# Four of the first layer's six modulation vectors as weighted sums on VectorE, spread over the attention phase, in place of TensorE products

## Chip, cores and metric

One NeuronCore of a Trainium2 chip. The metric is the device time of one execution in microseconds; lower is better. The kernel runs in float32 throughout; its large products are made of three products of float32r parts.

## What is computed

Two layers over 512 latent and 256 context tokens of width 1024. Each layer is modulated by six vectors, made from the conditioning `c` (for the latent tokens) and `c_ctx` (for the context):

```python
for layer in range(DEPTH):
    mod_x = silu_c @ ada_w[layer] + ada_b[layer]      # 1024 -> 6 x 1024
    mod_c = silu_cc @ ada_w[layer] + ada_b[layer]
    sh1, sc1, g1, sh2, sc2, g2 = split(mod_x, 6)
    hx = modulate(rmsnorm(x, norm1_g[layer]), sh1, sc1)
    mx, mc = hybrid_mixer(hx, hc, ...)                # projections, two kinds of attention heads, gates
    x = x + g1 * (mx @ w_out[layer])
    hx = modulate(rmsnorm(x, norm2_g[layer]), sh2, sc2)
    x = x + g2 * squared_relu_mlp(hx, w_mlp1[layer], w_mlp2[layer])
```

and the same for the context in the first layer. The first two vectors (shift and scale of the first norm) are wanted at the start; the third only when the mixer's output is projected, the fourth and fifth at the second norm, the sixth at the end of the MLP's first part. The change concerns these last four, in the first layer.

## The kernel before

Tokens lie on the free axis, 128 features on the partitions. `build` makes a list of items, layer by layer, and `run` (L400) emits them in order; each engine then works through its own queue in that order, so the list is the schedule. Ahead of every item, and behind each one that uses weights, `advance` (L409) emits loads and splits of the next weight slabs: a slab of 128 x 1024 is loaded on SP's queue into one of four buffers of the pool `wraw`, and split into a high part (a cast on ScalarE, L244) and a low part (a subtraction, L245, on VectorE or, for a few slabs, on GpSimd). There are six pairs of split buffers (`NSPL`): a slab's split can be emitted only when the slab six places before it in the order of use has had its last use (L413).

The attention phase follows the hand-written table `SCHEDULE` (L109): 24 lines with one block of projections each, and the stages that run behind it. Its first eighteen lines begin

```python
vg0 g0A g2A g1A      # 1        gk1 g1O g0N g3B      # 8       ka1 r13 r01          # 15
vg1 g0B g1B g2B      # 2        qa0 g2qk g1N g3C     # 9       kb1 r1N r02          # 16
vg2 g1C g2C g0C      # 3        qb0 g2S g2K g3qk     # 10      g5 r03 r31           # 17
vr0 g0qk g1qk        # 4        ka0 g3S g3K g2D      # 11      g1 r32 r0N y5        # 18
vr1 g0S g0K g1S      # 5        kb0 g3D g2O          # 12
vr2 g0D g1K tabs     # 6        qa1 g3O g2N r11      # 13
gq1 g1D g0O g3A      # 7        qb1 r12 g3N          # 14
```

(the numbers are this document's). A block is some 48 to 144 matmuls and the evacuation of its banks; `vg` and `vr` (values, token-major, `tok_blocks` L735) use four slabs in all three of their blocks, slabs 5 to 8 and 9 to 12. A stage of the gated linear attention is a step of one head: A to C make the gate's prefix sums (VectorE and ScalarE), `qk` scales queries and keys (VectorE), S and K make scores and transposes (TensorE), D the states over the chunks (TensorE, then VectorE), O the output, N its norm. The retention heads' stages are r..1 to r..N.

The modulation vectors are made in three ways. Shift and scale of the first layer come first, in four quarters (L374). The first layer's other four vectors come in two groups of 2048 features: `ada_step` (L279) multiplies, for one of eight k tiles, four stretches of 512 columns of the raw weights by the conditioning's column pair (32 stationary columns, 30 of them zero), side by side in four strips of the array; with `ada_load` two raw slabs are loaded a step ahead. `ada_next` (L306) is placed behind each block of the schedule (L1132): 16 steps, behind the blocks 1 to 16. At a group's end `ada_finish` (L259) copies the bank to SBUF, transposes it on TensorE and adds the bias on VectorE. The second layer's six vectors are made by `ada_sums` (L324) during the first layer's MLP: for each k tile VectorE adds the raw slab, weighted by a per-partition scalar, to an accumulator, once for each of the two conditionings (L340 for the first k tile, L342 for the others); after eight tiles one product with a one-hot column adds up the partitions (L348), and `ada_finish` follows. Its accumulator shares a buffer with the retention tables (`tag="rtab"`).

```python
for v in range(2):
    c = cs[:, kk, v : v + 1]
    if kk == 0:
        nc.vector.tensor_scalar(acc[:, v], w, c, None, op0=ALU.mult)
    else:
        nc.vector.scalar_tensor_tensor(acc[:, v], w, c, acc[:, v], op0=ALU.mult, op1=ALU.add)
```

Of the kernel before, what the change touches and what calls it, by code (L numbers as in the profile page):

```python
# [16 lines left out]
P = 128  # L17
# [22 lines left out]
class Item:  # L40
    """A piece of the program: emits instructions; may need weight slabs; a stage runs one block after its deps."""
# [5 lines left out]
class Chains:  # L47
    """Instruction chains that hop between engines: each tick emits the next step of every chain under way.

    Queued chains start one per tick, with at most WIDTH of them under way."""  # L50
# [45 lines left out]
class Act:  # L96
    """A moving operand in two float32r parts, made by chains for token ranges."""
# [10 lines left out]
# one block of projections and the attention stages that run behind it, per line; at most NSLOT tiles live  # L108
# [30 lines left out]
def build(ctx: ExitStack, tc, a):  # L139
# [7 lines left out]
    tp = ctx.enter_context(tc.tile_pool(name="tab", bufs=1))  # L147
    mp = ctx.enter_context(tc.tile_pool(name="mp", bufs=NSLOT))
# [23 lines left out]
    def bc(col, n):  # L172
        """[P, c] -> [P, c, n], each value repeated n times."""
        return col.rearrange("p (c o) -> p c o", o=1).to_broadcast([col.shape[0], col.shape[1], n])

    def rep(tab, c):
        """[P, n] -> [P, c, n], the row repeated c times."""
        return tab.rearrange("p (o t) -> p o t", o=1).to_broadcast([tab.shape[0], c, tab.shape[1]])
# [5 lines left out]
    # ---- constants and inputs  # L184
# [32 lines left out]
    # silu(c) of both vectors, as 32 stationary columns (30 of them zero) per k tile  # L217
# [14 lines left out]
    # ---- weight slabs: [128, 1024] and its exact split into two float32r parts  # L232
# [14 lines left out]
    class RankSlab(Slab):  # L247
        """Four copies of 32 columns per k tile: the second one's low part, the others' high parts."""
# [7 lines left out]
    # ---- adaLN vectors: mod[l][p, v, j] for feature 128 j + p  # L256
    mod = [const.tile([P, 2, 48], F32, name=f"mod{l}") for l in range(DEPTH)]

    def ada_finish(l, pt, tiles, n, fold=1):  # L259
        """pt: row 32 c + v holds, for vector v, n features from the tile tiles[c] on; `fold` such parts are summed."""  # L260
# [18 lines left out]
    def ada_step(state, l, g, kk):  # L279
        if kk == 0:  # L280
            state["pt"] = psa.tile([P, 512], F32, tag="psa", name=f"ada_{l}_{g}")
        pt = state["pt"]
        w = state.pop("w", None)
        if w is None:
            w = ada_load(l, g, kk)
        for c in range(4):
            nc.tensor.matmul(
                pt[32 * c : 32 * c + 32, :], cs[:, kk, :], w[c // 2][:, (c % 2) * 512 : (c % 2 + 1) * 512],
                start=(kk == 0), stop=(kk == KK - 1),
            )  # L290
        if kk == KK - 1:
            state["end", l, g] = ch.start(ada_finish(l, pt, [16 * g + 4 * c for c in range(4)], 512))

    def ada_load(l, g, kk):
        ws = []
        for i in range(2):
            w = wraw.tile([P, WCOL], F32, tag="raw", name=f"adaw_{l}_{g}_{kk}_{i}")
            c0 = g * 2048 + i * WCOL
            nc.sync.dma_start(w, a["ada_w"][l, kk * P : (kk + 1) * P, c0 : c0 + WCOL])
            ws.append(w)  # L300
        return ws

    ada_state = {}
    ada_queue = [(l, g, kk) for l, g in ((0, 1), (0, 2)) for kk in range(KK)]

    def ada_next():  # L306
        if ada_queue:
            l, g, kk = ada_queue.pop(0)
            ada_step(ada_state, l, g, kk)
            if ada_queue:  # L310
                ada_state["w"] = ada_load(*ada_queue[0])

    def ada_drain(l, g):
        while any(q[:2] == (l, g) for q in ada_queue):
            ada_next()
        ch.finish(ada_state["end", l, g])

    # the second layer's: weighted sums over the k tiles on the vector engine, one product to add the partitions
# [5 lines left out]
    def ada_sums(l):  # L324
        acc = tp.tile([P, 2, WCOL], F32, tag="rtab", name=f"adaacc_{l}")
        todo = [(u, kk) for u in range(6) for kk in range(KK)]
# [8 lines left out]
        for i, (u, kk) in enumerate(todo):  # L335
# [8 lines left out]
            if kk == KK - 1:  # L344
# [7 lines left out]
                ada_state["end", l] = ch.start(ada_finish(l, pt, [8 * u + 2 * c for c in range(4)], 256))  # L352
                yield

    # the first layer's shift and scale, in four quarters of 256 features each
# [18 lines left out]
    def quarter(q, middle=None, end=None):  # L374
        """Shift and scale of a quarter, even and odd k tiles apart."""
# [65 lines left out]
    def project(pt, slab, c0, acts, t0, t1, ks=None, first=0, last=None):  # L441
        """pt[:, :t1 - t0] += W[:, tile].T @ act over the k tiles `ks` of a slab part [kk, 128]."""
# [14 lines left out]
    # ---- RMSNorm over features, for a group of tokens at a time  # L457
    class Norm:
# [3 lines left out]
        def square(self, kk, t0, t1, first):  # L462
            """A chain that adds a tile's squares to the sum."""
# [14 lines left out]
        def late_square(self, kk, t0, t1):  # L478
            """A tile's squares that the product over the partitions adds to the sum."""
            sq = temp(f"sq_{self.name}_{kk}_{t0}")[:, 0 : t1 - t0]  # L480
            nc.scalar.activation(sq, xs[kk][:, t0:t1], AF.Square)
            self.late.append(sq)
# [40 lines left out]
        def apply_all(self, l, shift, v, t0, t1, ks=range(KK)):  # L523
            """Chains that make the tiles `ks` of a group of tokens."""
# [910 lines left out]
```

## Time and profile before

| | us |
|---|---|
| median of three runs | 1659.46 |
| lowest, highest run | 1658.64, 1659.53 |
| span of the profiled execution, first to last instruction | 1658.9 |

The profile's time is its span; the runs shown lie from 0.3 below to 0.6 above it. PE is TensorE's matmul, PEld its weight load, DVE VectorE, ACT ScalarE, POOL GpSimd, SP the engine whose queue issues most loads. A granted clock of 1.00 is 2.4 GHz, 0.50 is 1.2 GHz. A row names the line of the program that made the instruction; where a helper records many operations, the tile names tell them apart (`ps_vr` is a bank of a `vr` block, `adaw` a raw slab of modulation weights, `lo_wi` a low part of an input-projection slab).

### The profile page before, as it was taken

The numbers are of one execution on the slowest core, as the hardware profiler recorded it, in microseconds if no ns is written. First come the engines' busy times: TensorE is split into PE (matmuls) and PEld (weight loads), VectorE is DVE, ScalarE is ACT, GpSimd is POOL, SyncE is SP. The second block draws the span as 40 slices with busy tenths as digits, with TensorE's granted clock in tenths as the row PEclk, the third lists the DMA queues.
The fourth block names the chain that finished last, engine by engine and source line by source line (L and its number), as shares of the span: only waits on it lengthen the run. The fifth ranks groups of instructions, "written<-read, shape, count | busy, mean of one in ns | idle before, by whom it ended". The sixth has DMA issues, their size and how long they took to land. (4 is left out here: it accounts for less than half of the span.)

```text
span 1658.9 us, 22890 instructions
## 1 busy us (share of the span) xinstructions
PE 1618.7 (98%) x9236; PEld 1384.2 (83%) x9236; DVE 946.9 (57%) x1491; ACT 629.5 (38%) x1083; POOL 201.6 (12%) x215
## 2 busy tenths in 40 slices
PE   5999999999999999999999999999999899999997
PEld 3778888888998888888888887888889888888887
DVE  5676664554755555555556476588466633443445
ACT  5535424562532222222212246363464532222232
POOL 3200021110111010110101121001110211010010
PEclk9999999999999999999999999999999999999999
DMA  9533433122323333333333222121123323223321
GB/s 323 175 127 126 137 108 102 39 88 90 103 89 127 115 127 109 120 102 116 126 115 127 95 88 66 51 77 52 51 89 128 103 89 102 91 100 102 102 64 51
DMA packets 57610, 173.80 MB, mean 105 GB/s; under 512 B 6208, under 2 KB 17792, under 8 KB 57504
## 3 DMA queue, kind: packets, MB, share of 16 engines
q1 hardware_dynamic: 55232, 164.85, 30.2%
q0 software_dynamic: 2272, 7.50, 1.2%
q8 instruction: 72, 1.18, 0.3%
q14 instruction: 34, 0.28, 0.0%
HBM read 168.13 MB, written 4.19 MB: 104 GB/s over the span
## 5 line engine op out<-in xcount | busy, mean ns | idle before, releaser
L437 PE MATMUL pm<-yh,hi_m 128*128 128x512 f32 (+1 forms) x800 | 279.6, 349 | 0.0
L437 PE MATMUL pm<-hidh,hi_m 128*128 128x512 f32 (+1 forms) x800 | 279.1, 349 | 0.0
L438 PE MATMUL pm<-yl,hi_m 128*128 128x512 f32 (+1 forms) x800 | 278.6, 348 | 0.0
L438 PE MATMUL pm<-hidl,hi_m 128*128 128x512 f32 (+1 forms) x800 | 278.4, 348 | 0.0
L439 PE MATMUL pm<-yh,lo_m 128*128 128x512 f32 (+1 forms) x800 | 278.2, 348 | 0.0
L439 PE MATMUL pm<-hidh,lo_m 128*128 128x512 f32 (+1 forms) x800 | 277.2, 347 | 0.0
L1208 ACT ACTIVATE relu<-pm 128x512 f32<-128x512 f32 (+1 forms) x100 | 51.1, 511 | 497.6 <-PE pm L439 493.9
L1212 DVE TENSOR_TENSOR hidl<-relu,hidh 128x512 fp32r<-128x512 f32 (+1 forms) x100 | 60.5, 607 | 296.0 <-POOL relu L1210 296.0
L1210 POOL TENSOR_TENSOR relu<-relu 128x512 f32<-128x512 f32 (+1 forms) x100 | 89.2, 893 | 760.3 <-ACT hidh L1209 760.2
L535 DVE SCALAR_TENSOR_TENSOR x<-pm,mod,x 128x512 f32<-128x512 f32 (+1 forms) x200 | 117.6, 640 | 106.6 <-PE pm L439 106.6
L437 PEld LDWEIGHTS pm<-yh,hi_m 128*128 128x128 f32 x800 | 152.6, 191 | 20.2 <-issue 1.2
L437 PEld LDWEIGHTS pm<-hidh,hi_m 128*128 128x128 f32 x800 | 151.5, 189 | 21.3 <-issue 1.1
L438 PEld LDWEIGHTS pm<-yl,hi_m 128*128 128x128 f32 x800 | 152.5, 191 | 18.8
L439 PEld LDWEIGHTS pm<-yh,lo_m 128*128 128x128 f32 x800 | 152.4, 191 | 19.0
L439 PEld LDWEIGHTS pm<-hidh,lo_m 128*128 128x128 f32 x800 | 151.1, 189 | 19.6
L438 PEld LDWEIGHTS pm<-hidl,hi_m 128*128 128x128 f32 x800 | 151.4, 189 | 18.9 <-issue 0.2
L245 DVE TENSOR_TENSOR lo_m<-raw_m,hi_m 128x1024 fp32r<-128x1024 f32 x126 | 154.0, 1222 | 10.6 <-ACT hi_m L244 10.6
L244 ACT CAST hi_m<-raw_m 128x1024 fp32r<-128x1024 f32 x128 | 129.6, 1040 | 51.6 <-DMA raw_m<-in_w_mlp 31.0
L342 DVE SCALAR_TENSOR_TENSOR adaacc<-adaw,cs,adaacc 128x1024 f32<-128x1024 f32 x84 | 103.9, 1278 | 0.0
L245 DVE TENSOR_TENSOR lo_wi<-raw_wi,hi_wi 128x1024 fp32r<-128x1024 f32 x49 | 60.6, 1249 | 29.8 <-ACT hi_wi L244 29.8
L437 PE MATMUL pwo<-yh,hi_wo 128*128 128x256 f32 (+1 forms) x224 | 70.9, 316 | 0.1
L438 PE MATMUL pwo<-yl,hi_wo 128*128 128x256 f32 (+1 forms) x224 | 70.3, 314 | 0.3 <-DVE yl L1056 0.3
(304 smaller groups left out, 2951.5 us busy)
## 6 DMA issues: line engine op xcount, KB each, us to landing
raw_m<-in_w_mlp SPq DMA_DIRECT2D x128, 512.0 KB, 3.5
adaw<-in_ada_w SPq DMA_DIRECT2D x80, 512.0 KB, 3.9
raw_wi<-in_w_in SPq DMA_DIRECT2D x58, 512.0 KB, 4.3
adaw<-in_ada_w SPq DMA_DIRECT2D x32, 256.0 KB, 6.3
raw_wo<-in_w_out SPq DMA_DIRECT2D x16, 512.0 KB, 3.4
x<-in_xT POOLq DMA_DIRECT2D x8, 384.0 KB, 7.8
x<-in_xT SPq DMA_DIRECT2D x8, 256.0 KB, 4.9
raw_wob<-in_w_out SPq DMA_DIRECT2D x4, 512.0 KB, 4.3
```

Of the source, the lines that this page charges most:

```text
L244: nc.scalar.copy(self.hi, self.raw)
L245: self.engine.tensor_sub(self.lo, self.raw, f32(self.hi))
L342: nc.vector.scalar_tensor_tensor(acc[:, v], w, c, acc[:, v], op0=ALU.mult, op1=ALU.add)
L437: nc.tensor.matmul(out, wh, xh, start=first, stop=False)
L438: nc.tensor.matmul(out, wh, xl, start=False, stop=False)
L439: nc.tensor.matmul(out, wl, xh, start=False, stop=last)
L535: nc.vector.scalar_tensor_tensor(xs[kk][:, t0:t1], pt[:, 0 : t1 - t0], mod[l][:, v, gate + kk : gate + kk + 1], xs[kk][:, t0:t1], op0=ALU. ...
L1208: nc.scalar.activation(r, pt[:, 0 : t1 - t0], AF.Relu)
L1210: nc.gpsimd.tensor_mul(r, r, r)
L1212: nc.vector.tensor_sub(a_.lo[:, t0:t1], r, f32(a_.hi[:, t0:t1]))
```

## The change

`ada_step` and `ada_load` go. `ada_sums` takes a list of vectors and makes the first layer's vectors 2 to 5 as well, its accumulator in a pool of its own (8 KB per partition; the descriptor scratch of the software DMA queue shrinks to 2 KB). `ada_next` runs its next step. There are nine steps to a vector: eight that emit a load for the step after and two sums, and one that emits the product over the partitions. A step is placed behind each block, as before, and one more at the end of each line of the schedule. `ada_drain` waits for one vector: the third ahead of the output projection, the fifth at the second norm, the sixth in the MLP's first part.

```diff
+    adap = ctx.enter_context(tc.tile_pool(name="adap", bufs=1))
...
-    def ada_step(state, l, g, kk):
-        if kk == 0:
-            state["pt"] = psa.tile([P, 512], F32, tag="psa", name=f"ada_{l}_{g}")
...
-        for c in range(4):
-            nc.tensor.matmul(
-                pt[32 * c : 32 * c + 32, :], cs[:, kk, :], w[c // 2][:, (c % 2) * 512 : (c % 2 + 1) * 512],
-                start=(kk == 0), stop=(kk == KK - 1),
-            )
...
-    ada_queue = [(l, g, kk) for l, g in ((0, 1), (0, 2)) for kk in range(KK)]
-
-    def ada_next():
-        if ada_queue:
-            l, g, kk = ada_queue.pop(0)
-            ada_step(ada_state, l, g, kk)
-            if ada_queue:
-                ada_state["w"] = ada_load(*ada_queue[0])
...
-    def ada_sums(l):
-        acc = tp.tile([P, 2, WCOL], F32, tag="rtab", name=f"adaacc_{l}")
-        todo = [(u, kk) for u in range(6) for kk in range(KK)]
+    def ada_sums(l, us=range(6)):
+        acc = adap.tile([P, 2, WCOL], F32, tag="acc", name=f"adaacc_{l}")
+        todo = [(u, kk) for u in us for kk in range(KK)]
...
-                ada_state["end", l] = ch.start(ada_finish(l, pt, [8 * u + 2 * c for c in range(4)], 256))
+                ada_state["end", l] = ada_state["end", l, u] = ch.start(
+                    ada_finish(l, pt, [8 * u + 2 * c for c in range(4)], 256)
+                )
                 yield
...
+    def ada_next():
+        if "sums0" not in ada_state:
+            ada_state["sums0"] = ada_sums(0, range(2, 6))
+        next(ada_state["sums0"], None)
+
+    def ada_drain(l, u):
+        while (l, u) not in [k[1:] for k in ada_state if k[0] == "end" and len(k) == 3]:
+            ada_next()
+        ch.finish(ada_state["end", l, u])
...
                 if it.slabs and l == 0:
                     plan.append(Item("ada", ada_next))
+            if l == 0:
+                plan.append(Item("ada", ada_next))
             seen.update(row)
...
-                        ada_drain(0, 2)
+                        ada_drain(0, 4)
...
-            plan.append(Item("ada1", lambda: ada_drain(0, 1)))
+            plan.append(Item("ada1", lambda: ada_drain(0, 2)))
...
+                if l == 0 and u == 0 and jps == [0]:
+                    ada_drain(0, 5)
...
-    nc = _bacc.Bacc("TRN2", target_bir_lowering=False, num_devices=1)
+    nc = _bacc.Bacc("TRN2", target_bir_lowering=False, num_devices=1, dynamic_dma_scratch_size=2048)
```

## Rows read from the trace of the kernel before

In order of time a row is: start in us, length in us, engine, line, operation, output and inputs by the program's names, partitions x elements and type, the number of instructions merged in it, and in square brackets the idle time before it with what ended it. In stretches a row is: start and end in us, their length, then for each engine the busy us and (x) the instructions in it, the granted TensorE clock as a share of 2.4 GHz, the DMA share and GB/s.

**Rows 1.** The page's busy line: us, share of the span, instructions.

```profile
PE 1618.7 (98%) x9236; PEld 1384.2 (83%) x9236; DVE 946.9 (57%) x1491; ACT 629.5 (38%) x1083; POOL 201.6 (12%) x215
```

**Rows 2.** Stretches behind blocks 2 to 8: busy us, granted clock, DMA.

```profile
88.29:100.40 12.11, 12.11 (x58) 9.09 (x57) 11.68 (x17) 1.55 (x8) 0.00 (x0) 1.00 0.27 87
100.40:112.50 12.10, 12.10 (x57) 9.09 (x56) 5.47 (x13) 10.28 (x17) 0.00 (x0) 1.00 0.52 180
112.50:124.61 12.11, 12.11 (x57) 9.09 (x56) 9.64 (x23) 0.00 (x0) 0.80 (x4) 1.00 0.47 168
124.61:140.59 15.98, 15.98 (x111) 12.56 (x110) 6.09 (x16) 4.69 (x8) 0.00 (x0) 1.00 0.21 67
140.59:152.14 11.55, 11.55 (x75) 9.59 (x74) 10.94 (x30) 8.44 (x23) 0.00 (x0) 1.00 0.51 184
152.14:166.02 13.88, 13.88 (x95) 11.92 (x94) 8.66 (x18) 9.40 (x18) 0.00 (x0) 1.00 0.46 148
166.02:179.97 13.95, 13.95 (x89) 11.47 (x88) 6.57 (x13) 6.57 (x13) 0.00 (x0) 1.00 0.24 80
```

**Rows 3.** TensorE's weight loads in block 4 (vr0), in order of time.

```profile
101.39 0.19 PEld L437 LDWEIGHTS ps_vr<-hi_wi,hh_n 128*128 128x128 f32 x1 [0.84 <-issue]
...
104.26 0.19 PEld L438 LDWEIGHTS ps_vr<-lo_wi,hh_n 128*128 128x128 f32 x1
```

**Rows 4.** TensorE's matmuls around two of the removed steps.

```profile
87.97 0.39 PE L439 MATMUL ps_vg<-hi_wi,hl_n 128*128 128x512 f32 x1
...
89.29 0.50 PE L437 MATMUL ps_vg<-hi_wi,hh_n 128*128 128x512 f32 x1
...
124.29 0.39 PE L439 MATMUL ps_vr<-hi_wi,hl_n 128*128 128x512 f32 x1
...
125.61 0.37 PE L857 MATMUL psf<-gq,gk 64*128 64x128 f32 x1
```

**Rows 5.** TensorE's matmuls around a product over partitions, second layer.

```profile
544.45 0.28 PE L439 MATMUL pm<-hidh,lo_m 128*128 128x256 f32 x1
...
545.65 0.50 PE L437 MATMUL pm<-yh,hi_m 128*128 128x512 f32 x1
```

**Rows 6.** VectorE's pair of weighted sums, second layer, and the next.

```profile
488.13 2.47 DVE L342 SCALAR_TENSOR_TENSOR adaacc<-adaw,cs,adaacc 128x1024 f32<-128x1024 f32 x2
490.52 1.22 DVE L245 TENSOR_TENSOR lo_m<-raw_m,hi_m 128x1024 fp32r<-128x1024 f32 x1
```

**Rows 7.** VectorE in order of time, behind blocks 1 to 4.

```profile
85.22 0.95 DVE L811 TENSOR_TENSOR gl<-gl,gt 128x768 f32<-128x768 f32 x1
...
99.35 0.96 DVE L821 TENSOR_TENSOR gt<-gt,gst 128x768 f32<-128x768 f32 x1
102.26 2.36 DVE L245 TENSOR_TENSOR lo_wi<-raw_wi,hi_wi 128x1024 fp32r<-128x1024 f32 x2 [1.95 <-ACT hi_wi L244]
...
120.30 0.68 DVE L757 TENSOR_REDUCE vsum<-ps_vr 128x4 f32<-128x512 f32 x1
...
121.22 1.13 DVE L760 TENSOR_SCALAR vr<-ps_vr,vsum 128x128 f32<-128x128 f32 x4
```

**Rows 8.** Stretches of 2 us around a stand of TensorE, second layer.

```profile
1292.00:1294.00 2.00, 0.73 (x7) 0.53 (x5) 1.52 (x4) 0.95 (x2) 0.00 (x0) 1.00 0.17 51
...
1296.00:1298.00 2.00, 0.84 (x3) 0.75 (x3) 2.00 (x2) 0.46 (x2) 1.58 (x2) 0.50 0.13 25
...
1302.00:1304.00 2.00, 2.00 (x17) 2.00 (x16) 1.75 (x5) 1.48 (x4) 0.00 (x0) 0.83 0.02 6
```

**Rows 9.** VectorE's last evacuation of qa0, TensorE's first matmul of qb0.

```profile
182.72 0.69 DVE L939 TENSOR_TENSOR rq<-ps_qa,c_sinT 64x512 f32<-64x512 f32 x1
...
182.18 0.58 PE L437 MATMUL ps_qb<-hh_n,hi_wi 128*128 128x512 f32 x1
```

**Rows 10.** VectorE's last evacuation of g1, TensorE's first matmul of g6.

```profile
303.01 0.42 DVE L1047 TENSOR_TENSOR sg<-se,ps_g 128x256 f32<-128x256 f32 x1 [0.48 <-ACT se L1046]
...
303.48 0.56 PE L437 MATMUL ps_g<-hh_n,hi_wi 128*128 128x512 f32 x1
```

More of the change, by code (lines that the diff above doesn't have):

```diff
@@ L277, in ada_finish @@
             )
-    def ada_step(state, l, g, kk):
-        if kk == 0:
-            state["pt"] = psa.tile([P, 512], F32, tag="psa", name=f"ada_{l}_{g}")
[L282 to L285, printed above, removed]
-        for c in range(4):
-            nc.tensor.matmul(
-                pt[32 * c : 32 * c + 32, :], cs[:, kk, :], w[c // 2][:, (c % 2) * 512 : (c % 2 + 1) * 512],
-                start=(kk == 0), stop=(kk == KK - 1),
-            )
[L291 to L301, printed above, removed]
-    ada_state = {}
-    ada_queue = [(l, g, kk) for l, g in ((0, 1), (0, 2)) for kk in range(KK)]
-    def ada_next():
-        if ada_queue:
-            l, g, kk = ada_queue.pop(0)
-            ada_step(ada_state, l, g, kk)
-            if ada_queue:
-                ada_state["w"] = ada_load(*ada_queue[0])
[L313 to L316, printed above, removed]
+    ada_state = {}
     onehot = const.tile([P, 2, 32], F32, name="onehot")
```

## The prediction, made before the change was built

> **What bounds the kernel now.** The page's busy line comes first: TensorE 98% of the span, VectorE 57% [rows 1]. Read alone, that says that work taken from TensorE and given to VectorE is a gain. An average over 1659 us can't be trusted here, since the change acts between 74 and 305 us only, so the second view cuts this stretch at the ends of the projection blocks. I number the blocks as the lines of SCHEDULE: vg0 is 1, vg1 2, vg2 3, vr0 4, vr1 5, vr2 6, and so on to g1, 18. In every piece TensorE is busy throughout at a granted clock of 1.00 (its 2.4 GHz level) and VectorE is not full [rows 2]: TensorE bounds this phase, and VectorE is ahead of it. But VectorE's share differs: 11.7 of 12.1 us behind block 2, 5.5 behind block 3, 10.9 of 11.6 behind block 6 [rows 2]. Where it is almost full, nothing more fits.
>
> **What goes.** Sixteen steps, one behind each of the blocks 1 to 16. The matmuls of a block follow each other by 0.22 us (13 of them between the two rows of [rows 3]). Around the step behind block 2 the distance is 89.29 - 87.97 = 1.32, so the step costs 1.1; where another plain float32 product follows, as behind block 5, it is 125.61 - 124.29 = 1.32 again, less the pace and some 0.1 for the change of format, which stays: 1.0 [rows 4]. Four steps of the first kind and twelve of the second: 4 x 1.1 + 12 x 1.0 = 16.4 us of TensorE, all on the path.
>
> **What comes.** Per vector a product over the partitions behind the sums: the second layer's same product moves the next matmul from 544.45 to 545.65, less the 256-column pace of 0.12, so 1.1 at most, 1.05 taken [rows 5]; four are 4.2. The transposes that follow are eight as before (four vectors by two, two groups by four): nothing. Alone, TensorE would end 16.4 - 4.2 = **12.2 us** earlier.
>
> VectorE gets 32 pairs of weighted sums. A pair holds it 490.52 - 488.13 = 2.4 us [rows 6]; the first pair of each vector is a plain product and cheaper, so some 28 x 2.4 + 4 x 1.4 = 73 us. Two steps come with each block: one right behind it, before the stages, and one behind the stages. With nine steps to a vector (eight sums, one product), all are spent with block 18.
>
> Priced at nothing: the 32 loads of 512 KB are 32 as before, now one to a step, on SP's queue; what hides them is that each is issued a step ahead, and if that cover were gone VectorE would wait some 4 us a step (the heavy rival below). The smaller descriptor scratch touches only POOL's DMAs, of which none is issued in this stretch; a delay of theirs would show at the start or where x is reloaded. The accumulator's own pool adds no instruction.
>
> **Who waits.** VectorE works its queue in order, so what stands behind the sums is late. I follow it by blocks. "Shift" is TensorE's time against before.
>
> *Block 4 (vr0), slabs 11 and 12.* They take the split buffers of slabs 5 and 6, which block 3 still reads; so their subtractions are emitted behind block 3, behind all of block 2's stages. Before, those stages run on VectorE without a gap from 85.22 to 99.35 + 0.96 = 100.3, and the two subtractions at 102.3 come just in time: vr0 begins at 101.39 and wants slab 11's low part at 104.26, less than a microsecond after it is made [rows 3, 7]. After: a sum behind block 1's stages, one behind block 2, 15.1 us of stages, one more sum, then the subtraction: 85.2 + 2.4 + 2.4 + 15.1 + 2.4 + 1.2 = 108.7. TensorE, three steps lighter, asks at 104.26 - 3.3 = 101.0. It stands **7.7 us** (bounds 6 and 9: whether the sums slip into small gaps or add some).
>
> *The clock.* In the second layer TensorE stood some 4.4 us (1292.7 to 1297.2 by the busy time); the granted clock was 0.50, the 1.2 GHz level, from then until about 1302.4 [rows 8]. 5.2 us of work at half rate gave 2.6 us away. A stand of 7.7 us is longer, so I take 2.6 again (bounds 0, if the clock holds, and 3.3, for the whole low stretch).
>
> *Block 5's product (vector 2).* From slab 12's subtraction, at 109.9, VectorE has what it had before in the pieces behind blocks 3 and 4 (5.5 - 2.4 and 9.6 less the 2.0 of vr1's first evacuation, together 10.8 [rows 2, 7]) and four sums, 9.6: free at 130.3. TensorE ends block 5 at 124.5 - 4.4 + 7.7 + 2.6 = 130.4. No stand here; had the clock held, it would be 2.5. Either way the shift behind this product is -5.4 + 7.7 + 2.6 + 1.0 = +5.9. In the piece behind block 5 VectorE has 6.1 us of work in 16 [rows 2] and catches up.
>
> *Blocks 6 to 8.* Block 8's stage reads at once head 1's states, made behind block 7. From 140.5 + 5.9 = 146.4 on VectorE has the 10.9 us behind block 6, of the 8.7 behind block 7 all but a subtraction (1.2) and a gate evacuation (1.1), and three sums [rows 2, 6]: 10.9 + 6.4 + 7.2, so 170.9. TensorE asks at 166.0 + 5.9 - 2.0 = 169.9. It stands **1.0** (0 to 3).
>
> *Block 9's product (vector 3).* This one is emitted behind block 9's stages, with no block between the last sum and it. VectorE's queue from block 6's end to that sum: 10.9 + 8.7 + 6.6, the evacuation of qa0 until 183.4, 3.4 into its piece, and seven sums of 2.4: 46.4, so 146.4 + 46.4 = 192.8 [rows 2, 9]. TensorE is there at 182.2 - 4.0 + 5.9 + 1.0 = 185.1 [rows 9]. It stands **7.7** (4 if VectorE carries no backlog into the block, 10 if its waits on ScalarE are not swallowed), and the clock falls again: 2.6 (0 to 3.3).
>
> *Blocks 10 to 17.* The evacuations and stages leave room, vector 4's product has a whole block between it and its last sum: nothing (0 to 2, in the range).
>
> *Block 18's product (vector 5)* is of the second kind again. VectorE ends g1's evacuation at 303.4 and then sums, 305.8; TensorE is past the stages at 303.5 in the same time base [rows 10]: **2.3** (0 to 5).
>
> **Sum:** -12.2 + 7.7 + 2.6 + 1.0 + 7.7 + 2.6 + 2.3 = +11.7 us. Nothing later gives this back, as TensorE bounds the rest too. The profiled span is 1658.9, the median 1659.46; the half microsecond between them lies around the span and stays. 1659.5 + 11.7 = **1671 us**. Its own range, not all ends at once: 1663 to 1681.
>
> **Rivals.** *All hidden.* Mechanism: VectorE's many short waits take in the sums, slab 11's low part is there when vr0 asks. It decides at that subtraction: a backlog below 1 us at block 3's end. For it: 57% busy [rows 1], 6.1 us of 16 behind block 5. Against: 11.7 of 12.1 behind block 2 [rows 2], just where it would have to fit. 1659.5 - 12.2 = 1647. The Trainium skill, "Perfetto Trace Analysis", section "Identifying the Most-Contended Engine", has the engine with the highest occupancy relieved first, and TensorE is that one; by that rule the time would be this 1647. The pieces between blocks speak against using it on the whole span.
>
> *Cancelled.* Only vr0's stand and its clock cost stay, the products find their sums done: -12.2 + 7.7 + 2.6 = -1.9, 1658. For it: the product of vector 4 shows the placing can work. Against: two products have no block before them.
>
> *Clock holds.* The stands without the low clock, but 2.5 at block 5: -12.2 + 7.7 + 2.5 + 1.0 + 7.7 + 2.3 = +9.0, 1668.
>
> *Heavy.* A buffer for the next load comes free only with VectorE's own late subtraction, and sums wait for their data: upper ends of the terms, -12.2 + 9 + 3.3 + 3 + 10 + 3.3 + 5 = +21, 1681, or a little over.
>
> **Chances.** This kernel's runs can tell 0.2%, 3.3 us, from no change. Forecast 0.45, clock holds 0.2, heavy 0.13: slower 0.78. Cancelled 0.09: same. All hidden 0.13: faster. The range leaves out the hidden case and what lies over the heavy one: 1656 to 1683.
>
> **What would show it.** The chain of waits of the changed kernel: weight loads of vr0 waiting for VectorE's subtraction, some 8 us once; the two products of vectors 3 and 5 waiting for the accumulator, 8 and 2 us; a granted clock of 0.50 for some 5 us behind the long ones; VectorE near full behind blocks 2 to 4 and 6 to 9. The forecast is wrong if TensorE stays busy through vr0, if the order of the subtractions on VectorE isn't the one I read from the code, or if the stands are there but a later part runs shorter.

## The result, and the profile after

| | before | after |
|---|---|---|
| median of four runs, us | 1659.49 | 1674.67 |
| lowest, highest run | 1658.64, 1659.65 | 1673.1, 1675.34 |
| span of the profiled execution | 1658.9 | 1673.3 |

The changed kernel is slower by 0.87% (ratio 1.0087, 95% interval 1.0075 to 1.01), 15.2 us, where 11.7 were forecast. Its line numbers lie some 25 lower from the removed functions on: the split is L245 and L246, the sums L304 and L306, the product over the partitions L312, the blocks' matmuls L413 to L415.

The page's busy line of the changed kernel answers to [rows 1]:

```profile
PE 1613.1 (96%) x9172; PEld 1386.9 (83%) x9172; DVE 1024.7 (61%) x1563; ACT 629.5 (38%) x1085; POOL 205.8 (12%) x215
```

TensorE did 5.6 us less, and VectorE, at 61% still far from full by this line, 77.8 more; the time rose. The line can't tell where. The changed kernel's waits of TensorE between 60 and 340 us can (engine and line waiting, for whom: us in total, times, longest):

```profile
PE ada L312 <- DVE adaacc L306: 8.5, 4, 6.8
PE ps_vr L414 <- DVE lo_wi L246: 8.2, 1, 8.2
PE po L879 <- DVE gl L869: 2.7, 3, 1.5
PE prk L946 <- DVE rq L915: 0.9, 1, 0.9
PE psb L833 <- DVE vr L736: 0.3, 1, 0.3
```

Before, TensorE was busy throughout the stretches behind blocks 2 to 8 [rows 2]. Now it has waits, all for VectorE. TensorE's instructions in order of time have them at their places: vr0's first product with slab 11's low part, then the products of vectors 2, 3 and 5 (in brackets the idle time and what ended it):

```profile
111.23 0.80 PE L414 MATMUL ps_vr<-lo_wi,hh_n 128*128 128x512 f32 x1 [8.22 <-DVE lo_wi L246]
133.13 0.64 PE L312 MATMUL ada<-adaacc,onehot 128*32 128x256 f32 x8 [0.37 <-DVE adaacc L306]
...
195.65 2.28 PE L312 MATMUL ada<-adaacc,onehot 128*32 128x256 f32 x16 [6.80 <-DVE adaacc L306]
...
316.82 0.64 PE L312 MATMUL ada<-adaacc,onehot 128*32 128x256 f32 x8 [0.81 <-DVE adaacc L306]
318.01 0.64 PE L312 MATMUL ada<-adaacc,onehot 128*32 128x256 f32 x8 [0.56 <-DVE adaacc L306]
```

Why slab 11 is late stands in VectorE's own order of time in the changed kernel (answering to [rows 7]): the stages of block 2, one pair of sums, the two subtractions, with no gap at all. Further down, the last sum of vector 3 comes behind the whole evacuation of qa0:

```profile
106.69 0.96 DVE L797 TENSOR_TENSOR gt<-gt,gst 128x768 f32<-128x768 f32 x1
107.56 2.48 DVE L306 SCALAR_TENSOR_TENSOR adaacc<-adaw,cs,adaacc 128x1024 f32<-128x1024 f32 x2
109.96 2.35 DVE L246 TENSOR_TENSOR lo_wi<-raw_wi,hi_wi 128x1024 fp32r<-128x1024 f32 x2
...
193.58 0.69 DVE L915 TENSOR_TENSOR rq<-ps_qa,c_sinT 64x512 f32<-64x512 f32 x1
194.31 2.48 DVE L306 SCALAR_TENSOR_TENSOR adaacc<-adaw,cs,adaacc 128x1024 f32<-128x1024 f32 x2
```

The stretches of the changed kernel around vr0's stand (12 us each, then one of 2 us right behind it) and vector 3's (2 us; columns as in [rows 2]):

```profile
88.00:100.00 12.00, 12.00 (x55) 9.94 (x54) 11.83 (x13) 2.91 (x13) 0.00 (x0) 1.00 0.28 87
100.00:112.00 12.00, 3.78 (x16) 2.84 (x15) 11.76 (x17) 8.49 (x15) 0.00 (x0) 0.85 0.08 23
112.00:124.00 12.00, 12.00 (x48) 9.74 (x47) 11.66 (x26) 2.10 (x2) 0.00 (x0) 0.87 0.76 269
...
112.00:114.00 2.00, 2.00 (x7) 1.52 (x6) 2.00 (x3) 0.42 (x1) 0.00 (x0) 0.50 0.84 256
...
190.00:192.00 2.00, 0.00 (x0) 0.00 (x0) 2.00 (x3) 1.97 (x4) 0.00 (x0) 1.00 0.32 49
192.00:194.00 2.00, 0.00 (x0) 0.00 (x0) 1.96 (x4) 0.28 (x1) 0.00 (x0) 0.93 0.92 320
196.00:198.00 2.00, 1.88 (x17) 0.35 (x9) 2.00 (x3) 0.01 (x1) 0.00 (x0) 0.50 0.20 27
198.00:200.00 2.00, 2.00 (x5) 1.62 (x6) 1.96 (x6) 1.31 (x2) 0.00 (x0) 0.50 0.63 236
200.00:202.00 2.00, 2.00 (x9) 1.59 (x9) 1.04 (x1) 0.00 (x0) 0.00 (x0) 0.87 0.00 0
```

From block 2's end to block 5's VectorE had 26.8 us of work in 36.3, in the middle piece 5.5 in 12 [rows 2]; from 88 to 124 us it now has 35.3 in 36. There it is the bound, whatever the page's 61% say. Behind each long stand the granted clock is at 0.50 (112 to 114 and 196 to 200 us).

### The profile page after: what moved, and what is told of

Read it like the earlier page. It is cut to its first block, busy times and chain, and to the rows that moved or that the text cites. A ratio compares the mean times of both kernels' runs of the same rounds, so it can differ in the third digit from the quotient of the medians.

```text
span 1673.3 us, 22855 instructions
## 1 busy us (share of the span) xinstructions
PE 1613.1 (96%) x9172; PEld 1386.9 (83%) x9172; DVE 1024.7 (61%) x1563; ACT 629.5 (38%) x1085; POOL 205.8 (12%) x215
## 5 line engine op out<-in xcount | busy, mean ns | idle before, releaser
L413 PE MATMUL pm<-yh,hi_m 128*128 128x512 f32 (+1 forms) x800 | 279.4, 349 | 0.0
L413 PE MATMUL pm<-hidh,hi_m 128*128 128x512 f32 (+1 forms) x800 | 279.1, 349 | 0.0
L415 PE MATMUL pm<-yh,lo_m 128*128 128x512 f32 (+1 forms) x800 | 278.0, 348 | 0.0
L415 PE MATMUL pm<-hidh,lo_m 128*128 128x512 f32 (+1 forms) x800 | 277.2, 347 | 0.0
L306 DVE SCALAR_TENSOR_TENSOR adaacc<-adaw,cs,adaacc 128x1024 f32<-128x1024 f32 x140 | 179.7, 1325 | 0.2
L413 PEld LDWEIGHTS pm<-yh,hi_m 128*128 128x128 f32 x800 | 152.4, 190 | 20.3 <-issue 1.2
L413 PEld LDWEIGHTS pm<-hidh,hi_m 128*128 128x128 f32 x800 | 151.4, 189 | 21.3 <-issue 1.1
L415 PEld LDWEIGHTS pm<-yh,lo_m 128*128 128x128 f32 x800 | 152.3, 190 | 19.0
L415 PEld LDWEIGHTS pm<-hidh,lo_m 128*128 128x128 f32 x800 | 151.1, 189 | 19.6
L246 DVE TENSOR_TENSOR lo_m<-raw_m,hi_m 128x1024 fp32r<-128x1024 f32 x126 | 154.0, 1222 | 10.6 <-ACT hi_m L245 10.6
L245 ACT CAST hi_m<-raw_m 128x1024 fp32r<-128x1024 f32 x128 | 129.7, 1041 | 49.5 <-DMA raw_m<-in_w_mlp 21.3
L246 DVE TENSOR_TENSOR lo_wi<-raw_wi,hi_wi 128x1024 fp32r<-128x1024 f32 x49 | 60.6, 1249 | 18.7 <-ACT hi_wi L245 18.5
L413 PE MATMUL pwo<-yh,hi_wo 128*128 128x256 f32 (+1 forms) x224 | 70.9, 316 | 0.1
```

Of the source, the lines that this page charges most:

```text
L245: nc.scalar.copy(self.hi, self.raw)
L246: self.engine.tensor_sub(self.lo, self.raw, f32(self.hi))
L413: nc.tensor.matmul(out, wh, xh, start=first, stop=False)
L415: nc.tensor.matmul(out, wl, xh, start=False, stop=last)
```

## The experiments

Each is timed, as a median, against the kernel before on the same chip. "Ahead" and "late" compare the start of the same block with the kernel before.

### Sums over 8 of 1024 columns

```diff
-                    nc.vector.scalar_tensor_tensor(acc[:, v], w, c, acc[:, v], op0=ALU.mult, op1=ALU.add)
+                    n = WCOL if l else 8
+                    nc.vector.scalar_tensor_tensor(
+                        acc[:, v, 0:n], w[:, 0:n], c, acc[:, v, 0:n], op0=ALU.mult, op1=ALU.add)
```

> The changed kernel, but the first layer's weighted sums run over 8 of the 1024 columns for the k tiles 1 to 7 (the rest of these four vectors is left out); loads, buffers, products over the partitions, drains and places in the order stay. Theory (the loss is VectorE's time and nothing else): the stands at vr0, at the products of vectors 2, 3 and 5 and at head 1's states vanish, with the low clock behind them; what is left is TensorE's saving of 12.2 us, so 1647, or 1649.5 if the 2.4 us by which the changed kernel is late before its first sum belong to the change. Rival (the loads, the accumulator's pool or the products themselves cost it): the time stays over 1665. What it measures besides: the term of 12.2 us by itself.

1652.1 us, ratio 0.9949 (0.9936 to 0.9961). So VectorE's time for the sums is worth 1674.7 - 1652.1 = 22.6 us; the loads, the buffers and the products, which all stay, do not make the kernel slower than before. The gain of 7.6 is less than the 10 to 12 expected, and TensorE's waits say why:

```profile
103.29 0.50 PE L417 MATMUL ps_vr<-lo_wi,hh_n 128*128 128x512 f32 x1 [1.88 <-DVE lo_wi L246]
...
178.81 1.07 PE L315 MATMUL ada<-adaacc,onehot 128*32 128x256 f32 x16 [2.38 <-DVE adaacc L307]
```

A lighter TensorE runs into VectorE's own work: 1.9 us at vr0, where the subtraction came just in time before [rows 3], and 2.4 at vector 3's product, whose tiny last sum still stands behind qa0's evacuation. Part of the 12.2 us was never to be had with this order.

### The side parts alone

```diff
+    adap = ctx.enter_context(tc.tile_pool(name="adap", bufs=1))
...
+    nc = _bacc.Bacc("TRN2", target_bir_lowering=False, num_devices=1, dynamic_dma_scratch_size=2048)
```

> The kernel before, with the change's two side parts alone: the descriptor scratch of 2 KB and a pool of its own for the accumulator of the second layer's sums. The changed kernel is 2.4 us late at its second block, before any sum can have delayed anything, with the granted clock lower at the start. Theory A (these 2.4 us differ from execution to execution and are not the change's): 1659.5 within 1. Theory B (the smaller scratch delays GpSimd's loads at the start, or of x later): 1661 to 1663.

1660.47, ratio 1.0003 (0.9994 to 1.0012): theory A, these parts cost nothing. The lateness itself is 2.55 us at block 1 (66.09 against 63.54) and 0.74 at block 2 (78.05 against 77.31), where the saved step should have made the changed kernel 1.1 early. It differs from execution to execution: in the kernels whose TensorE instructions up to block 2 are the changed kernel's, that block began between 74.3 and 78.2 us. Why the changed kernel's profiled execution is among the late ones isn't shown.

### Slabs 11 and 12 split by GpSimd

```diff
-        for j in (range(5, 9), (5, 6))[l]:
+        for j in ((5, 6, 7, 8, 11, 12), (5, 6))[l]:
             sl[j].engine = nc.gpsimd
```

> The changed kernel, but the low parts of slabs 11 and 12 are made by GpSimd, which is idle there, instead of VectorE; the sums and products stay where they are. In the changed kernel ScalarE's casts of both slabs end at 102.8 and TensorE asks for slab 11's low part at 103.0; GpSimd takes 2.5 us for such a subtraction, so the parts are there at about 104.3 and 106.8 and vr0 stands some 1.5 us instead of 8.2, with no low clock. Theory A (the sums of a vector are one queue, and TensorE that no longer waits at vr0 waits at vector 2's product): TensorE is at that product about 9 us earlier, VectorE ends the eighth sum only 2.4 us earlier, so a new stand of some 6 to 7 us with the low clock behind it appears there; 1674.7 less about 2, 1671 to 1674. Theory B (each stand is a loss of its own): the 8.2 and the 2.6 of the clock are won, 1664 to 1666.

1676.1, ratio 1.0097 (1.0083 to 1.0111): nothing won, where theory A had some 2 us. TensorE's waits in order of time:

```profile
105.07 0.78 PE L414 MATMUL ps_vr<-lo_wi,hh_n 128*128 128x512 f32 x1 [1.91 <-POOL lo_wi L246]
134.40 2.28 PE L312 MATMUL ada<-adaacc,onehot 128*32 128x256 f32 x16 [8.33 <-DVE adaacc L306]
```

The waits are those of theory A: vr0's stand fell from 8.2 to 1.9, and the product of vector 2, which had stood 0.4, stood 8.3. The two stands are one backlog, met at the first thing that TensorE wants behind it.

### Products only behind a block

```diff
             if kk == KK - 1:
+                while not ada_state.get("block", True):
+                    yield
...
             if l == 0:
-                plan.append(Item("ada", ada_next))
+                plan.append(Item("ada", lambda: ada_next(False)))
```

> The changed kernel, but a product over the partitions is emitted only behind a block of projections, never at a line's end: vector 2's stays behind block 5, vector 3's moves from the end of line 9 to behind block 10, vector 4's from behind block 14 to behind block 15, vector 5's from behind block 18 to behind block 20, as the steps behind it slip. The sums on VectorE are the same number. Theory (a product with no block between it and its last sum stands for VectorE's queue): vector 3's stand of 6.8 us and the low clock behind it (2.6) go, and the 2 us at vector 5's; 1674.7 - 11.4 = 1663, within 3. Rival (VectorE's backlog passes into the next thing that TensorE wants from it, the evacuation of qa0's banks or the heads' stages): at least 1670. vr0's stand of 8.2 us stays in both.

1666.6, ratio 1.0044 (1.0031 to 1.0056): 8 us of the 11.4 expected, just outside theory and rival. (Behind the start of block 2 the two traces differ by 6.2; the rest lies in the head, which differs between executions.) The waits for the accumulator are gone from the list; vr0's 8.2 is as it was:

```profile
PE ps_vr L418 <- DVE lo_wi L246: 8.2, 1, 8.2
PE po L883 <- DVE gl L873: 3.7, 3, 1.8
PE ps_g L417 <- DVE sg L1027: 1.4, 1, 1.4
```

The wait of heads' outputs for their states grew by 1.0 (2.7 in the changed kernel) and a gate's evacuation came 1.4 late: the backlog passes on in part. The larger part is won, since behind block 10 VectorE is done with the sums when TensorE asks.

### A stand filled with work

```diff
                 pt = psa.tile([P, 512], F32, tag="psa", name=f"ada_{l}_{u}")
+                if l == 0 and u == 3:
+                    for _ in range(14):
+                        nc.tensor.matmul(pt[:, 0:256], late["delta"], late["cosT"][:, 0:256], start=True, stop=True)
```

> The changed kernel, with 14 plain float32 products of 128 x 256 (of two constant tables, into the bank of vector 3's product, which then overwrites them) emitted on TensorE right ahead of vector 3's product, so that TensorE works through most of its stand of 6.8 us there; by the 16 products over partitions' kind of rows they take about 0.43 us each, 6.0 in all (an estimate). Nothing else changes, and VectorE ends the last sum when it did. Theory (the low clock behind a stand comes from TensorE having nothing to do, and is a cost beside the stand): the granted clock stays near 1.00 from 192 to 202, the product takes 1.1 us in place of 2.3 and the next six matmuls 1.4 in place of 2.7; 1674.7 - 2.5 = 1672.2. Rival (the clock falls whatever TensorE does there, or what is won is lost at the next thing that waits for VectorE): 1674.7 within 1, or more.

1671.83, ratio 1.0073 (1.0059 to 1.0087), 2.8 less than the changed kernel. The stretches of 2 us behind the product of vector 3, which here began at 192.2:

```profile
190.00:192.00 2.00, 1.40 (x7) 0.90 (x5) 1.95 (x3) 0.00 (x0) 0.00 (x0) 1.00 0.67 229
192.00:194.00 2.00, 1.26 (x17) 0.37 (x17) 2.00 (x3) 0.00 (x0) 0.00 (x0) 1.00 0.02 6
194.00:196.00 2.00, 2.00 (x12) 1.66 (x10) 2.00 (x4) 1.32 (x2) 0.00 (x0) 1.00 0.79 244
196.00:198.00 2.00, 2.00 (x11) 1.65 (x10) 1.53 (x4) 0.00 (x0) 0.00 (x0) 1.00 0.05 18
```

The clock stayed at 1.00. From qa0's first matmul to ka0's the kernel lost 6.9 us against the one before, the changed kernel 8.5: 1.6 is the clock's share shown in the traces (the product itself stood twice more, 0.8 and 0.6, between its parts). The intervals of the two ratios overlap, so the 2.8 by itself proves nothing, and what exceeds the 1.6 isn't settled. The Trainium skill, "TensorE: Matmul & The Clock Gate", section "What's actually happening", has the array at half rate behind idle time and at full rate behind work; the two traces agree.

### Steps from block 4 on

```diff
-                if it.slabs and l == 0:
+                if it.slabs and l == 0 and "vr0" in seen | set(row):
                     plan.append(Item("ada", ada_next))
-            if l == 0:
+            if l == 0 and "vr0" in seen | set(row):
                 plan.append(Item("ada", ada_next))
```

> The changed kernel, but the steps begin behind block 4 (vr0) instead of block 1, so that no sum stands ahead of the subtractions of slabs 11 and 12 on VectorE; all 36 steps are spent by line 21. Theory: vr0's stand (8.2 us) and its low clock (2.6) go; the product of vector 2 comes behind block 8 with its last sum before that block and does not stand; vector 3's comes at the end of line 12, vector 5's at the end of line 21, both with no block before them: 2 to 6 us and 1 to 3 us. 1659.5 - 12.2 + 0 to 2.4 (the head) + 1.5 (head 1's states) + 2 to 6 + 1 to 3 = 1652 to 1660. Rival (vr0's stand comes from the slabs' loads or ScalarE's casts, which are as late): the 8 us stay at vr0, 1665 or more.

1682.62, ratio 1.0139 (1.0123 to 1.0154): a miss, 8 us slower than the changed kernel. vr0's wait fell to 1.1, as the theory has it, and ka0 began 0.9 ahead of before; but the products met the same queue elsewhere:

```profile
164.44 1.85 PE L312 MATMUL ada<-adaacc,onehot 128*32 128x256 f32 x12 [3.91 <-DVE adaacc L306]
...
227.37 1.08 PE L312 MATMUL ada<-adaacc,onehot 128*32 128x256 f32 x8 [4.84 <-DVE adaacc L306]
229.58 1.08 PE L312 MATMUL ada<-adaacc,onehot 128*32 128x256 f32 x8 [1.13 <-DVE adaacc L306]
...
359.42 2.28 PE L312 MATMUL ada<-adaacc,onehot 128*32 128x256 f32 x16 [5.82 <-DVE adaacc L306]
```

Vector 2's product even had a block before it (block 8) and stood 3.9: one block is not enough where VectorE is more than one block behind.

### The sums spread out

This kernel and the five behind it place the steps by a table (line: behind its block, at its end; L is a load, S a sum, P the product). Three shorter tables do the same between the parts of the output projection (`WO_STEPS`, `WOB_STEPS`) and the MLP's first tiles.

```diff
+    STEPS = {3: ('L', 'S'), 5: ('L', 'S'), 8: ('L', 'S'), 12: ('', 'L'), 13: ('SL', 'S'), 14: ('L', 'SL'),
+             15: ('SL', 'S'), 16: ('PL', 'SL'), 17: ('SL', 'S'), 18: ('L', 'SL'), 19: ('SL', 'S'), 20: ('L', 'SL'),
+             21: ('S', ''), 22: ('PL', 'SL'), 23: ('SL', 'SL'), 24: ('SL', 'SL')}
...
```

> The changed kernel with the same sums and products in other places: three sums in the lines 1 to 12 (at the ends of lines 3, 5 and 8), one or two a line from line 13 on, the last of vector 4 between the blocks of the output projection's first token group, vector 5's between those of the second group and the MLP's first tiles; a load is issued one place ahead of its sum, and every product stands behind a block with at least one block between it and its last sum. Theory (only VectorE's backlog in lines 1 to 12 and the products without a block before them cost time): no stand for the accumulator and none of over 2 us at vr0, so the kernel is at least as fast as the one with narrow sums, 1652.1, less the 2.4 us that it still stood at a product: 1648 to 1653, faster than both kernels. Rival (the sums only move the backlog to the second norm and the MLP's first tiles, where VectorE makes the norm's two parts): a stand of 5 us or more there, 1656 or over.

1689.05, ratio 1.0175 (1.0161 to 1.0188): a miss, but right up to block 17. There it is 15.4 us ahead: the sixteen steps (16.4) less one product (1.05); that it fits to the tenth is in part luck, as the head differs between executions. Then all is lost: 7.9 from block 20 to the output projection, 3.1 of them between the starts of blocks 20 and 21, and more behind. TensorE's long waits:

```profile
389.64 2.27 PE L320 MATMUL ada<-adaacc,onehot 128*32 128x256 f32 x16 [8.38 <-DVE adaacc L312]
...
461.19 1.22 PE L483 MATMUL st_n<-ssum_n,ones_d 128*128 128x256 f32 x2 [8.21 <-DVE ssum_n L466]
...
488.13 2.28 PE L320 MATMUL ada<-adaacc,onehot 128*32 128x256 f32 x16 [4.86 <-DVE adaacc L312]
```

The rival names the last two. The first is in the output projection, which begins with four parts of 18 matmuls and four of 6; vector 4's last sums and its product stood among these, and TensorE was through them before VectorE was through the sums. No sum of this kernel waited for its load by more than 0.15 us; the next expectation's words that some did are not borne out.

### Two or three vectors, the others by TensorE

```diff
                 if it.slabs and l == 0:
+                    plan.append(Item("ada", pe_next))
...
```

`pe_next` is `ada_step` for vectors 4 and 5 (or, over 256 columns a strip, for 5 alone).

> Vectors 2 and 3 as weighted sums, vectors 4 and 5 by eight TensorE steps behind the blocks 1 to 8 as the kernel before has them. The 16 sums stand in lines 13 to 24, each load one place ahead, the product of vector 2 behind block 18, that of vector 3 behind the second block of the output projection, a whole block between each and its last sum. In the kernel with the sums spread out TensorE was 15.4 us ahead at block 17 and lost it all later, where sums stood between the output projection's short blocks and the MLP's first tiles and waited for loads; here no sum stands there. Theory: eight steps (8.2 us) go, two products (2.1) come, nothing stands: 1659.7 - 6.1 = 1653.6, up to 0.9 more for the later start of the first block that the changed programs showed: 1653 to 1656. Rival (sums in the lines 18 to 24 delay the gates' evacuation, and blocks wait for their banks): 1657 or over.

> Vectors 2, 3 and 4 as weighted sums, vector 5 by eight narrower TensorE steps (four strips of 256 columns, about 0.5 us each, an estimate from the product over partitions: 8 matmuls of 256 columns for 1.05 us) behind the blocks 1 to 8. The 24 sums: seven in lines 1 to 12, 17 in lines 13 to 24; products behind blocks 14 and 20 and behind the output projection's third block. Theory: 16.4 go, 3.2 and 4.4 come, nothing stands: 1659.7 - 8.8 = 1650.9, up to 0.9 more; 1650 to 1653. Rival (24 sums are already too many for VectorE's room in lines 4 to 12 and 19 to 24): stands of 1 to 3 us each at vr0, at head 1's and 3's stages and at the gates' evacuation, 1655 to 1662.

1666.81 (ratio 1.0039, 1.0027 to 1.0052) and 1664.13 (1.0023, 1.0014 to 1.0032): both slower than before, both misses. With two vectors the kernel was 6.0 us ahead at the output projection, as worked out (6.1), and lost 13.6 from there to the MLP, most of it at one place:

```profile
378.88 2.28 PE L320 MATMUL ada<-adaacc,onehot 128*32 128x256 f32 x16 [7.20 <-DVE adaacc L312]
```

7.2 of stand, 1.05 for the product, 1.1 of waits for the last gated outputs ahead of it; most of the rest lies behind the stand, where the granted clock was 0.50 from 376 to 385 us. With three it was 3.7 ahead and lost 9.2 in the same way. So the products were moved behind the projection's tenth part, with the table changed for three vectors:

```diff
-    WO_STEPS = ['', 'P', '', '', '', '', '', '', '', '', '', '']
+    WO_STEPS = ['', '', '', '', '', '', '', '', '', 'P', '', '']
```

> The kernel with two vectors summed, but the product of vector 3 behind the tenth short or full block of the output projection instead of the second. With the product behind the second, TensorE was 6.0 us ahead where the output projection begins and then stood 7.2 us at that product, since its last sums on VectorE stand behind the last gates, with the granted clock at 0.50 from 376 to 385: 13.6 us lost in all. Theory (the stand is the product's place alone): the 6.0 us stay to the end, 1654 within 2, faster than before by 0.25 to 0.45%. Rival (TensorE runs ahead of VectorE at the start of the output projection anyway, and the next thing that waits for VectorE, the residuals' banks, takes the stand over): 1660 or more.

> The kernel with three vectors summed, the 24 sums moved ahead by about one line (8 in lines 1 to 12, none behind block 24's last stage), the products behind blocks 13 and 19 and behind the output projection's tenth block. Theory: the 4.7 us at vector 4's product with its low clock (9.2 in all) go, and the 4.3 us lost around vector 3's product, where its transposes waited for ScalarE's copy, go in part: 1650.9 to 1655. Rival (24 sums are too many for the room in lines 19 to 24): vector 4's stand goes, but the gates' evacuation is late: 1656 to 1660.

1658.22 (ratio 0.9989, 0.998 to 0.9998) and 1657.69 (0.9985, 0.9976 to 0.9994): no stand for the accumulator, but both miss their theory; the first lies between theory and rival, the second in its rival's range. With three vectors the kernel was 7.8 us ahead at the output projection and lost 5.0 by the MLP's first product. The product is 1.05 of it; TensorE's groups in the output projection (three vectors) show 2.3 more, for the last gated outputs, made late behind the last sums; the remaining 1.6 isn't accounted for:

```profile
L453 PE MATMUL pwo<-yh,hi_wo 128*128 128x512 f32 (+1 forms) x73 | 28.3, 388 | 1.3 <-ACT yh L1070 1.3
L454 PE MATMUL pwo<-yl,hi_wo 128*128 128x512 f32 (+1 forms) x72 | 27.5, 381 | 1.0 <-DVE yl L1072 1.0
```

Last, with two vectors, the sums ended at block 22 and the product behind block 24:

> The kernel with two vectors summed and two made by TensorE's eight steps, the 16 sums between line 10 and block 22 and the products behind blocks 17 and 24, so that no sum stands ahead of the last gates (blocks 23 and 24) and none near the output projection. With sums to the end of line 24 the kernel was 6.6 us ahead where the output projection begins and lost 5.5 until the second norm: 1.05 for the product, 2.8 of waits for the last gated outputs, which VectorE makes behind the sums. Theory: the 2.8 and what follows them go; 6.1 us are won to the end, 1653.6 to 1655, 0.3 to 0.4% faster than before. Rival (two sums in lines 13 to 15 and 19 to 21 are too many behind VectorE's own work there): stands of 1 to 3 us, 1657 to 1660.

1667.1, ratio 1.0046 (1.0032 to 1.006): a miss. 3.1 were lost between the starts of blocks 20 and 21, as with all sums spread out (3.1). In the first three-vector kernel it was 4.2, but there vector 3's product (1.05) and a wait of its transposes for ScalarE (1.7) lie in the same place. These three kernels have two sums in line 19; the others with such a table, which lost nothing there, have one. The first pair of the line fell beside GpSimd's products and took 4.5 to 4.6 us in place of 2.5 in all three (the last section has why), and in the two kernels without a product there TensorE then waited 1.3 and 1.1 for the gate's evacuation (this kernel's rows):

```profile
309.42 4.56 DVE L312 SCALAR_TENSOR_TENSOR adaacc<-adaw,cs,adaacc 128x1024 f32<-128x1024 f32 x2
```

```profile
323.20 0.70 PE L801 MATMUL hs<-pr,ones_v 128*128 128x256 f32 x2 [1.33 <-DVE sg L1066]
325.01 0.67 PE L456 MATMUL ps_g<-hh_n,hi_wi 128*128 128x512 f32 x1 [1.11 <-DVE sg L1066]
```

And the finish of the last product met another engine:

```profile
372.73 0.69 PE L269 MATMUL adat<-c_ident,adarow 128*128 128x128 f32 x2 [6.60 <-ACT adarow L264]
```

The product's transposes stand in TensorE's queue ahead of the output projection, and they wait for ScalarE's copy of the product's bank, behind the last gates in its own queue. The best version found, three vectors with late products, is 0.15% faster than the kernel before: its interval leaves out 1, but the gain is less than the 0.2% that the prediction called measurable.

## Why the prediction was right

The forecast held by its own steps: TensorE bounds the phase, VectorE's queue is what it waits for, and the stands came where they were foretold. Against its terms:

- **What goes.** 16.4 less a product of 1.05 is 15.35; with the sums out of the way up to block 17, 15.4 was measured (from block 2 on, where the head no longer counts, 14.4 against 14.25).
- **Block 4, slabs 11 and 12**: forecast 7.7, measured 8.2. The subtraction ended at 111.2 where 108.7 was worked out, but TensorE asked later too, at 103.0 and not 101.0, as its head was late. That VectorE is the cause was shown by the small sums (1.9 left).
- **The clock**: forecast 2.6 twice. From block 4's first matmul to the first score (-1.5 to +8.1 against before) 9.6 us are lost: 8.2 + 0.4 + 1.05 for vector 2's product - 2.05 for two steps leaves 2.0. From qa0 to ka0 8.5 are lost: 6.8 + 1.05 - 2.0 leaves 2.65. The filled stand showed 1.6 of it directly. *Clock holds* is refuted by the row at 0.50.
- **Block 5's product**: no stand forecast, 0.4 measured. The condition of the prediction, that a stand would come if TensorE arrived earlier, was shown by the split on GpSimd: 8.3.
- **Blocks 6 to 8**: forecast 1.0, measured 1.5. **Block 9's product**: 7.7, measured 6.8. **Block 18's**: 2.3, measured 0.81 + 0.56 = 1.4.
- **Blocks 10 to 17**: nothing forecast; three waits of heads' outputs and keys for VectorE of 0.5 to 0.9 (one of them ahead of block 9), 2.1 together. This is the term that failed: room in the stretch's sum is not room at each place. Ahead of the wait at 244.0 us (0.8) VectorE worked without a gap from 234.8, where a pair of sums took 1.0 longer beside GpSimd (last section); without this it would have been in time. The prediction has no such price.

Measured costs: 8.2 + 2.0 + 0.4 + 1.5 + 6.8 + 2.65 + 1.4 + 2.1 = 25.05; less the 12.2, +12.85 where the sum gave +11.7. Single terms miss by up to 2.1, in both directions, so the nearness of the sum is in part luck.

The profiled execution is 15.3 late where the output projection begins: 12.85, and 1.8 ahead of the first sum (0.7 late at block 2, where the saved step should have it 1.1 early); 0.6 isn't accounted for. In the second layer 0.85 come back, near 1002 and 1302 us, where the prediction had nothing given back, and the spans differ by 14.4. The medians differ by 15.2 because the profiled execution of the kernel before was a long one. Every run on record lasts 1.7 to 1.8 us longer than its span, so the span of 1658.9 belongs to a run of some 1660.7, 1.2 above the median (the changed kernel's lies 0.4 above its own); the prediction, which set it against the median with half a microsecond around it, took it for a typical one. Why the changed kernel's head is late isn't settled; the starts of block 2 lie up to 3.9 us apart in executions whose TensorE instructions up to there are the same, and the clock in the head is one thing that differs (10-us stretches, kernel before first, then the changed one):

```profile
30.00:40.00 10.00, 8.78 (x91) 5.35 (x90) 6.96 (x17) 6.25 (x12) 2.67 (x3) 1.00 1.09 350
60.00:70.00 10.00, 10.00 (x51) 8.44 (x50) 6.63 (x11) 5.81 (x13) 3.81 (x2) 0.99 0.36 105
```

```profile
30.00:40.00 10.00, 8.48 (x74) 5.03 (x76) 7.10 (x17) 5.40 (x10) 2.46 (x2) 0.83 1.09 350
60.00:70.00 10.00, 10.00 (x43) 8.46 (x44) 5.96 (x10) 5.94 (x12) 5.18 (x2) 0.80 0.34 109
```

The rival *All hidden* was not reached even with sums of 8 columns (1652, not 1647). *Cancelled* had the products find their sums done; vector 3's stood 6.8. *Heavy* had sums wait for their loads; in the changed kernel none did by more than 0.15 us. By the Trainium skill, "Perfetto Trace Analysis", section "Identifying the Most-Contended Engine", the engine with the highest occupancy is optimized first. Over the span this is TensorE; in the changed kernel's rows of 88 to 124 us it is VectorE, with 35.3 of 36 against TensorE's 27.8. Read by stretches, the same ranking names the other engine.

## What to carry to other kernels

Before work is moved from a full engine to a half-empty one, cut the phase at the places where the full engine asks the other for something, and count the other's queue up to each of them; a share over the span says nothing of these places. A removed wait comes back at the next such place unless the queue has had room in between, so an edit is worth trying only where that room can be pointed to. A consumer of a long row of sums belongs at least a whole block behind the last of them (one was too little behind block 8, where the queue was longer), and not at a change of phase, where the engine ahead runs dry.

## What had not been expected

A pair of sums takes 2.48 us alone. Beside GpSimd's products of rotary tables (two took 2.7 us before) both are slower. The changed kernel's rows of the two engines around 234 us:

```profile
234.80 3.52 DVE L306 SCALAR_TENSOR_TENSOR adaacc<-adaw,cs,adaacc 128x1024 f32<-128x1024 f32 x2
```

```profile
233.50 3.73 POOL L922 TENSOR_TENSOR rk<-rk,rw_k 128x512 f32<-128x512 f32 x2 [23.60 <-DVE rw_k L921]
```

Each loses 1.0 to 1.1 us: the two took turns, and together lasted 4.8 us, little less than one behind the other. Seven of the changed kernel's 64 sums ran beside such work and were some 7.6 us longer in all (an estimate, from their lengths against 1.28 us, or 0.73 for a first sum). That is one reason why VectorE's busy time grew by 77.8 us where 73 were counted. Slabs 11 and 12, split on GpSimd beside VectorE's stages, took 3.0 us each; the pair at 60 us took 2.6 each. The Trainium skill, "SBUF — State Buffer", section "SBUF: two separate sides", has GpSimd and a VectorE operation with two SBUF inputs share one pair of ports, which the one that starts first holds for its whole instruction; rows that are longer on both engines agree.
